# Pooling branch of a hybrid decoder mixer: means on ScalarE, ramp and subtraction on GpSimd, output matmuls at column tile 13

## The chip, the core and the metric

The kernel runs on one core of one Trainium2 chip. A core has five engines with a queue each: TensorE (PE, matmuls), VectorE (DVE), ScalarE (ACT), GpSimd (POOL) and SyncE (SP), which here issues the loads of all weights. Each engine works through its own queue in order and waits at semaphores for others. TensorE writes to PSUM (eight banks, handed out in this kernel by four pools, pa, pb, pt and pd); the other tiles lie in SBUF. The metric is the device time of one execution in microseconds (us).

## The reference

Two layers for 256 tokens of width 1,024 in float32. Each layer is a token mixer followed by a mixture of experts (32 experts, all of whose weights are streamed). The change touches the mixer, and of it the pooling branch:

```python
proj = h @ w_in[l]                                  # 1024 -> 3584 columns
u_conv = proj[..., :2 * D_CONV]                     # 2 x 512: the convolution branch
u_pool = proj[..., 2 * D_CONV:2 * D_CONV + D_POOL]  # 512: the pooling branch
gate_a, gate_b = jnp.split(jax.nn.sigmoid(proj[..., 2 * D_CONV + D_POOL:]), N_BRANCHES, axis=-1)
y_a = conformer_conv_branch(...)                    # GLU, 31 causal taps, layer norm, silu, w_conv_out
y_b = pool_branch(u_pool, pool_w[l], pool_scale[l])
x = x + g1[:, None, :] * ((gate_a * y_a + gate_b * y_b) @ w_out[l])

def pool_branch(u, pool_w, pool_scale):
    # four groups of 128 channels, windows 2, 4, 8, 16; at token s the count is min(s + 1, w)
    pooled = jnp.stack([causal_window_mean(ug[:, :, gi], w) for gi, w in enumerate(POOL_WINDOWS)], axis=2) - ug
    y = jnp.einsum("bsgc,gco->bsgo", pooled, pool_w).reshape(b, s, D_MODEL)
    return y * pool_scale
```

## The kernel before

Activations lie transposed, channels on the 128 partitions and 256 tokens along the free dimension. Weights come through a ring of 13 SBUF buffers of 1 MB (tiles `wt`, two more buffers `wx` during the experts), loaded by SP in a fixed stream; `done(key)` (L125) gives a buffer back and lets the next load be issued.

The projection is cut into 14 column tiles n = 0 to 13, each with two halves (L598 to L603). Matmuls on float32 weights are made of three faster ones: the weight is split into a rounded part `whi` (ScalarE, L444) and a residual `wlo` (GpSimd, for a few halves VectorE, L446), and `mm3` (L382) issues three matmuls for each product. `do_split(n + 2, hf)` prepares the half that comes two tiles later. The tiles run through the groups in the order 1, 0, 2, 5, 6, 3, 4 (L169), two tiles each: n = 0 to 3 is the convolution's input, n = 4 and 5 the pooling branch's (its result is `upad`, with 16 columns of zeros ahead), n = 6 to 9 the second gate (`mixed`), n = 10 to 13 the first (`ga`).

Between the halves stands the work of the two branches, in program order, since the four compute engines are scheduled by hand here (L587); only the queue of SP is ordered by the compiler's own scheduler.

- `conv` (L493) spreads 31 taps over four channel groups, 124 steps on VectorE (L503, L505), each multiplying a shifted window of `vpad` by a column and adding it to an accumulator in PSUM. The accumulators hold two of the three banks of the pool pd; the last four steps write `acc` in SBUF.
- `pool_sum(i)` (L513) builds window sums on GpSimd at n = 6 to 9, `pool_mean(i)` (L521) the means at n = 7 to 10 on VectorE: one instruction for the tokens from 16 on (L525), and for the first 16, where the count ramps up, a product with the reciprocals `rc16` (L528) and a subtraction (L529).
- `pool_out(m2)` (L531) multiplies by the pooling weights: two matmuls (L535) into a bank of pd (m2 even) or pt (m2 odd), read by two instructions of VectorE that merge them into `mixed` (L539). Two calls follow each half of n = 11.
- After n = 11 `flush` (L301) runs what is pending of the adaLN gate: two matmuls (L337) into pd, each copied by ScalarE into `gb` (L338). `gb` has the buffer that `upad` had.
- After n = 12 `ln_a` (L548) adds up `acc` on VectorE (tile `lt`, L544, L545) and takes the mean over channels by a matmul with ones (L551). `ln_b` (L558) stands within the last half of n = 13, `ln_c` (L572) behind it, after the first six matmuls of a later adaLN part (`lates`, L320). The rest of these covers the time until the layer norm's result (`ah`, `al`) is there for the matmuls with w_conv_out.

Of the kernel before, what the change touches and what calls it, by code (L numbers as in the profile page):

```python
# [7 lines left out]
F32 = mybir.dt.float32  # L8
# [4 lines left out]
AF = mybir.ActivationFunctionType  # L13
OP = mybir.AluOpType
# [4 lines left out]
P = 128  # L19
# [7 lines left out]
WINDOWS = (2, 4, 8, 16)  # L27
# [22 lines left out]
def trunk(ctx, tc, x, c, mixer_norm_g, w_ada, b_ada, w_in, conv_w, conv_b, conv_ln_g, conv_ln_b,  # L50
# [3 lines left out]
    nc = tc.nc  # L54
# [3 lines left out]
    two = ctx.enter_context(tc.tile_pool(name="two", bufs=2))  # L58
# [14 lines left out]
    def pd(shape):  # L73
        return psD.tile(shape, F32, name="pd", tag="pd")
# [50 lines left out]
    def done(key):  # L125
        finished.add(key)
        while state["done"] + 1 < len(stream) and stream[state["done"] + 1][0] in finished:
            state["done"] += 1
        issue()
# [104 lines left out]
    rc16 = cst.tile([P, 4, 16], F32, name="rc16")  # L234
# [152 lines left out]
    def mixer(l, mix, norm, g1):  # L387
# [7 lines left out]
        def transpose_x():  # L395
            hps.extend((pa, pb)[kp % 2]([P, 2, SEQ]) for kp in range(4))
            for tt in range(TT):
                v = xn[:, tt, :].rearrange("p (m k) -> p k m", k=KC)
                for k in range(KC):
                    nc.tensor.transpose(hps[k // 2][:, k % 2, tt * P:(tt + 1) * P], v[:, k, :], ident)  # L400
# [14 lines left out]
        def divide(kp):  # L415
            f = st["f", kp]
            ks = slice(2 * kp, 2 * kp + 2)
            nc.scalar.copy(hT[:, 0, ks, :], f)  # L418
            eng = nc.vector if kp in DIV_DVE else nc.gpsimd
            eng.tensor_tensor(hT[:, 1, ks, :], f, hT[:, 0, ks, :].bitcast(F32), op=OP.subtract)  # L420

        vpad = work.tile([P, 4, 30 + SEQ], F32, name="vpad")
        upad = work.tile([P, 4, 16 + SEQ], F32, name="upad", tag="gb")
        nc.gpsimd.memset(vpad[:, :, :30], 0.0)
        nc.gpsimd.memset(upad[:, :, :16], 0.0)
        st = {}
# [83 lines left out]
        def pw_of(i):  # L510
            return st["pw"][:, 3:7] if i % 2 else st["pw"][:, 0:4]

        def pool_sum(i):  # L513
            if i == 0:
                st["pw"] = work.tile([P, 7, n16], F32, name="pw", tag="hT")
            prev = pw_of(i - 1) if i else upad
            d = 1 << i
            lo = (1, 3, 7, 16)[i]
            nc.gpsimd.tensor_tensor(pw_of(i)[:, i:, lo:], prev[:, i:, lo:], prev[:, i:, lo - d:n16 - d], op=OP.add)

        def pool_mean(i):  # L521
            if i == 0:
                st["pooled"] = work.tile([P, 4, SEQ], F32, name="pooled", tag="t1")
            cur = pw_of(i)
            nc.vector.scalar_tensor_tensor(st["pooled"][:, i, 16:], cur[:, i, 32:], 1.0 / WINDOWS[i], upad[:, i, 32:],  # L525
                                           op0=OP.mult, op1=OP.subtract)
            f = two.tile([P, 16], F32, name="f16")
            nc.vector.tensor_tensor(f, cur[:, i, 16:32], rc16[:, i, :], op=OP.mult)  # L528
            nc.vector.tensor_tensor(st["pooled"][:, i, :16], f, upad[:, i, 16:32], op=OP.subtract)  # L529

        def pool_out(m2):  # L531
            pw = tiles["pw", l]
# [54 lines left out]
        with tc.manual_schedule(engines={E.PE, E.DVE, E.Activation, E.Pool}):  # L587
            transpose_x()
            for step in START[l]:
                if isinstance(step, tuple):  # L590
                    do_split(*step)
                elif step < 4:
                    modulate(step)
                else:
                    divide(step - 4)
            sg = work.tile([P, 4, SEQ], F32, name="sg", tag="t1")
            acc = mix.tile([P, 4, SEQ], F32, name="acc")
            for n in range(14):  # L598
                if n == 6:
                    st["mixed"] = work.tile([P, 8, SEQ], F32, name="mixed", tag="X0")  # L600
                if n == 10:
                    st["ga"] = work.tile([P, 8, SEQ], F32, name="ga", tag="hT")
                for hf in range(2):  # L603
                    mms(n, hf, ln_b if (n, hf) == (13, 1) else None)
                    if n == 0 and hf == 1:
                        vec_cols(l)
                    if n == 11:
                        for m2 in (2 * hf, 2 * hf + 1):
                            pool_out(m2)
                        if hf:  # L610
                            done(("pw", l))
                    if (n, hf) == (13, 1):
                        for _ in range(6):
                            next(lates)
                        ln_c()
                    conv(2 * n + hf)
                    if hf == 0 and 7 <= n <= 10:
                        pool_mean(n - 7)
                    do_split(n + 2, hf)
                    if hf == 0 and 6 <= n <= 9:  # L620
                        pool_sum(n - 6)
                if n == 12:
                    ln_a()
                evac(n)
                if n % 2:
                    flush(2 if n < 11 else None)
                if n == 0:
                    for _ in g1:
                        pass
                if n == 7 and l + 1 < DEPTH:  # L630
                    small_ada(l + 1)
            for _ in lates:
                pass
            mhl = work.tile([P, 2, 8, SEQ], F32R, name="mhl", tag="big")
            ah, al = st["ah"], st["al"]

            cps = [(pa if q % 2 == 0 else pb)([P, 2, SEQ]) for q in range(4)]
            mt4 = mix.tile([P, 4, SEQ], F32, name="mt4", tag="acc")

            def mixed_a(m2):  # L640
                for q in (2 * m2, 2 * m2 + 1):
                    t = mt4[:, q % 4, :]
                    nc.vector.scalar_tensor_tensor(t, cps[q // 2][:, q % 2, :], s["bo"][:, q:q + 1], st["ga"][:, q, :],
                                                   op0=OP.add, op1=OP.mult)
                    nc.gpsimd.tensor_tensor(t, st["mixed"][:, q, :], t, op=OP.add)

            def mixed_b(m2):
                for q in (2 * m2, 2 * m2 + 1):
                    t = mt4[:, q % 4, :]
                    nc.scalar.copy(mhl[:, 0, q, :], t)  # L650
                    nc.vector.tensor_tensor(mhl[:, 1, q, :], t, mhl[:, 0, q, :].bitcast(F32), op=OP.subtract)

            for i in range(2):
                for m in range(8):
                    hi, lo = sp[14 + i, m // 4]
                    ms = slice(m % 4 * P, (m % 4 + 1) * P)
                    for jj in range(2):
                        j = 2 * i + jj
                        mm3(cps[m // 2][:, m % 2, :], hi[:, jj, ms], lo[:, jj, ms], ah[:, j, :], al[:, j, :],
                            j == 0 and m % 2 == 0, j == 3)  # L660
                    if i == 1 and m % 2:
                        mixed_a(m // 2)
                        if m > 1:
                            mixed_b(m // 2 - 1)
                    if m % 4 == 3:
                        do_split(16 + i, m // 4)
                if i == 0:
                    flush()
            ps = [[pd([P, 512]), pd([P, 512])], [pd([P, 512]), pt([P, 512])]]

            def out_mm(i, tt, hs=range(2)):
                ts = slice(tt * P, (tt + 1) * P)
                for h in hs:
                    hi, lo = sp[16 + i, h]
                    for mm in range(2):
                        m = 2 * i + mm
                        mm3(ps[tt][h], mhl[:, 0, m, ts], mhl[:, 1, m, ts], hi[:, mm, :], lo[:, mm, :], m == 0, m == 7)

            def out_add(tt, hs=range(2)):
                for h in hs:  # L680
                    hs = slice(h * 512, (h + 1) * 512)
                    t = two.tile([P, 512], F32, name="ot", tag="part", bufs=3)
                    nc.vector.tensor_tensor(t, ps[tt][h], s["g1"][:, hs], op=OP.mult)
                    nc.vector.tensor_tensor(xs[:, tt, hs], xs[:, tt, hs], t, op=OP.add)

            for i in range(2):
                for tt in range(TT):
                    out_mm(i, tt)
                if i == 0:
                    do_split(18, 0)  # L690
                    do_split(18, 1)
                    mixed_b(3)
                    do_split(19, 0)
                    do_split(19, 1)
            router_prep(l)
# [555 lines left out]
```

## Time and profile before

| what | us |
|---|---|
| runs of the kernel before, median (lowest to highest) | 916.63 (912.15 to 921.05) |
| the profiled execution | 921.07 |
| its span, first to last instruction | 919.3 |
| busy: TensorE | 838.3 (91%) |
| busy: VectorE | 539.7 (59%) |
| busy: ScalarE | 287.2 (31%) |
| busy: GpSimd | 207.6 (23%) |
| moved by DMA | 298.35 MB, 325 GB/s in the mean |

The busy shares are means over stages of different kinds. In the experts' stages TensorE works almost without a pause while DMA streams at about 400 GB/s; in the mixers VectorE and GpSimd carry much more of the work. So the stretch around the change is read by itself: times in the rows are microseconds from the span's start, the mixer of layer 0 runs its column tiles from about 40 to 160, that of layer 1 from about 480 to 600.

### The profile page before, as it was taken

What the parts mean: (1) busy time and instruction counts of PE and PEld (TensorE: products, weight loads), DVE (VectorE), ACT (ScalarE), POOL (GpSimd) and SP (SyncE); (2) the same over time, 40 slices, a digit from 0 to 9 for tenths busy, and PEclk for the clock granted to TensorE, in tenths of its full rate; (3) what the DMA queues carried; (4) which work ended last, traced back from release to release, by engine and by line L of the source; (5) the groups of instructions that cost most, each with busy time, mean ns of one, the idle gap of its engine ahead of it and who ended that gap; (6) DMA issues with size and microseconds to landing.
All of it is one profiled execution on the core that took longest, in us unless ns stands there. A gap on an engine that the chain in (4) does not pass through costs nothing. (4 is left out here: it accounts for less than half of the span.)

```text
span 919.3 us, 12760 instructions
## 1 busy us (share of the span) xinstructions
PE 838.3 (91%) x4862; PEld 517.5 (56%) x4862; DVE 539.7 (59%) x1134; ACT 287.2 (31%) x462; POOL 207.6 (23%) x140
## 2 busy tenths in 40 slices
PE   4699939999998999999979993999899799999996
PEld 1489917864544544545349992787554454545442
DVE  2379993786443545454476999468644354535354
ACT  2254314633321222222135440364432122222222
POOL 1279912632000000000025892243200000000001
PEclk9699959999999999999989997899799999999998
DMA  9999734969999999999999752396699999999961
GB/s 349 368 365 395 282 109 146 375 239 357 408 408 407 407 400 313 406 408 409 403 373 384 280 173 102 122 402 227 221 352 409 360 357 409 409 409 409 359 225 46
DMA packets 100086, 298.35 MB, mean 325 GB/s; under 512 B 13941, under 2 KB 23461, under 8 KB 100010
## 3 DMA queue, kind: packets, MB, share of 16 engines
q1 hardware_dynamic: 99448, 296.30, 85.4%
q8 instruction: 44, 0.72, 0.3%
q10 hardware_dynamic: 434, 1.06, 0.3%
q14 instruction: 32, 0.26, 0.1%
q0 software_dynamic: 128, 0.02, 0.0%
HBM read 296.29 MB, written 1.05 MB: 323 GB/s over the span
## 5 line engine op out<-in xcount | busy, mean ns | idle before, releaser
L1095 PE MATMUL pb<-wt,XT 128*64 128x512 f32 x928 | 226.4, 592 | 0.0
L446 POOL TENSOR_TENSOR wlo<-wt,whi 128x1024 fp32r<-128x1024 f32 x60 | 147.2, 2464 | 140.2 <-ACT whi L444 117.2
L1095 PEld LDWEIGHTS pb<-wt,XT 128*64 128x64 f32 x928 | 72.8, 137 | 131.7 <-issue 129.0
L444 ACT CAST whi<-wt 128x1024 fp32r<-128x1024 f32 x80 | 83.0, 1049 | 99.1 <-PE pb L384 50.9
L505 DVE SCALAR_TENSOR_TENSOR pd<-vpad,cols,pd 128x256 f32<-128x256 f32 x232 | 108.0, 488 | 5.7
L1108 DVE SCALAR_TENSOR_TENSOR sl<-sl,ws,pb 128x256 f32<-128x256 f32 x32 | 15.4, 480 | 153.4 <-ACT sl L1107 153.4
L1055 DVE TENSOR_TENSOR xs<-xs,pd 128x512 f32<-128x512 f32 x124 | 84.2, 683 | 33.0 <-PE pd L1048 32.9
L1067 PE MATMUL pd<-wt,aT 128*64 128x512 f32 x448 | 102.3, 598 | 0.0
L1074 ACT CAST yhl<-y 128x512 fp32r<-128x512 f32 x64 | 39.5, 618 | 132.9 <-DVE y L1073 132.9
L1020 ACT ACTIVATE XT<-pa,B,A 128x256 f32<-128x256 f32 x112 | 57.1, 559 | 67.4 <-PE pa L1015 67.1
L383 PE MATMUL pa<-hhl,whi 128*128 128x256 f32 x224 | 68.8, 307 | 5.3 <-ACT hhl L418 5.3
L320 PE MATMUL pd<-wt,cb 128*32 128x512 f32 x384 | 55.4, 664 | 14.4 <-DMA wt<-in_w_ada_dram 14.4
L1078 DVE TENSOR_TENSOR yhl<-y,yhl 128x512 fp32r<-128x512 f32 x64 | 44.3, 692 | 41.1 <-ACT yhl L1074 41.0
L384 PE MATMUL pa<-hhl,whi 128*128 128x256 f32 x224 | 67.2, 300 | 0.3
L1107 ACT ACTIVATE sl<-pb 128x256 f32<-128x256 f32 x32 | 12.3, 384 | 175.4 <-PE pb L1095 160.0
L1015 PEld LDWEIGHTS pa<-G,xhl 128*128 128x128 f32 x448 | 62.4, 193 | 7.7 <-issue 2.7
L1015 PE MATMUL pa<-G,xhl 128*128 128x256 f32 x448 | 64.7, 288 | 2.2 <-issue 2.2
L385 PE MATMUL pa<-hhl,wlo 128*128 128x256 f32 x224 | 66.1, 295 | 0.5 <-POOL wlo L446 0.5
L383 PE MATMUL pb<-hhl,whi 128*128 128x256 f32 x224 | 63.6, 284 | 0.0
L384 PE MATMUL pb<-hhl,whi 128*128 128x256 f32 x224 | 62.7, 280 | 0.0
L385 PE MATMUL pb<-hhl,wlo 128*128 128x256 f32 x224 | 62.6, 279 | 0.0
L1047 PE MATMUL pd<-yhl,GT 128*128 128x512 f32 x124 | 56.1, 453 | 6.0 <-PEq L953 5.4
(251 smaller groups left out, 1353.8 us busy)
## 6 DMA issues: line engine op xcount, KB each, us to landing
wt<-in_w_expert_gate_dram SPq DMA_DIRECT2D x116, 512.0 KB, 8.2
wt<-in_w_expert_up_dram SPq DMA_DIRECT2D x116, 512.0 KB, 10.9
wt<-in_w_expert_down_dram SPq DMA_DIRECT2D x52, 1024.0 KB, 10.7
wt<-in_w_ada_dram SPq DMA_DIRECT2D x48, 1024.0 KB, 10.9
wt<-in_w_in_dram SPq DMA_DIRECT2D x28, 1024.0 KB, 13.6
wt<-in_w_out_dram SPq DMA_DIRECT2D x8, 1024.0 KB, 4.9
wx<-in_w_expert_down_dram SPq DMA_DIRECT2D x8, 1024.0 KB, 10.6
wx<-in_w_expert_gate_dram SPq DMA_DIRECT2D x12, 512.0 KB, 3.7
```

The lines of the kernel that those rows point to most:

```text
L383: nc.tensor.matmul(o, ah, bh, start=start, stop=False, skip_group_check=True)
L384: nc.tensor.matmul(o, ah, bl, start=False, stop=False, skip_group_check=True)
L385: nc.tensor.matmul(o, al, bh, start=False, stop=stop, skip_group_check=True)
L444: nc.scalar.copy(hi, wv)
L446: eng.tensor_tensor(lo, wv, hi.bitcast(F32), op=OP.subtract)
L505: nc.vector.scalar_tensor_tensor(acc[:, j, :] if t == CONV_K - 1 else a, src, w, a, op0=OP.mult, op1=OP.add)
L1015: nc.tensor.matmul(p[:, kk, :], xhl[:, q, tt, k * P:(k + 1) * P], Gs[ch][:, tt, :], start=i == 0, stop=i == 3)
L1020: nc.scalar.activation(XTs[ch][:, k, :], p[:, kk, :], AF.Identity, bias=s["B2"][:, k:k + 1], scale=s["A2"][:, k:k + 1])
L1047: nc.tensor.matmul(o, GTs[b][:, tt, :], ys[b][0][:, hs], start=True, stop=False)
L1055: nc.vector.tensor_tensor(xs[:, tt, hs], xs[:, tt, hs], outs.pop(part), op=OP.add)
L1067: nc.tensor.matmul(o[64 * j:64 * j + 64, :], aTs[b][:, h, 64 * j:64 * j + 64], wv[j][:, h, :], start=h == 0, stop=h == 1)
L1095: nc.tensor.matmul(p[64 * j:64 * j + 64], XT[:, k, so + 64 * j:so + 64 * j + 64], w[j][:, :, kk, :], start=k == 0, stop=k == KC - 1)
```

## The change

The mean of the tokens from 16 on is taken on ScalarE, a copy with a scale, into `pooled`. A new function `pool_diff`, called once after the second half of n = 10, does the rest on GpSimd: four products for the first 16 tokens and one subtraction of `upad` over all four groups, in place. The output matmuls of `pool_out` and the release of the pooling weights follow the halves of n = 13 instead of n = 11. `ga`, whose buffer the window sums `pw` use, is allocated one tile later.

```diff
         def pool_mean(i):
             if i == 0:
                 st["pooled"] = work.tile([P, 4, SEQ], F32, name="pooled", tag="t1")
-            cur = pw_of(i)
-            nc.vector.scalar_tensor_tensor(st["pooled"][:, i, 16:], cur[:, i, 32:], 1.0 / WINDOWS[i], upad[:, i, 32:],
-                                           op0=OP.mult, op1=OP.subtract)
-            f = two.tile([P, 16], F32, name="f16")
-            nc.vector.tensor_tensor(f, cur[:, i, 16:32], rc16[:, i, :], op=OP.mult)
-            nc.vector.tensor_tensor(st["pooled"][:, i, :16], f, upad[:, i, 16:32], op=OP.subtract)
+            nc.scalar.activation(st["pooled"][:, i, 16:], pw_of(i)[:, i, 32:], AF.Copy, scale=1.0 / WINDOWS[i])
+
+        def pool_diff():
+            v = st["pooled"]
+            for i in range(4):
+                nc.gpsimd.tensor_tensor(v[:, i, :16], pw_of(i)[:, i, 16:32], rc16[:, i, :], op=OP.mult)
+            nc.gpsimd.tensor_tensor(v, v, upad[:, :, 16:], op=OP.subtract)
...
-                if n == 10:
+                if n == 11:
                     st["ga"] = work.tile([P, 8, SEQ], F32, name="ga", tag="hT")
...
-                    if n == 11:
+                    if n == 13:
                         for m2 in (2 * hf, 2 * hf + 1):
                             pool_out(m2)
...
                     if hf == 0 and 6 <= n <= 9:
                         pool_sum(n - 6)
+                    if (n, hf) == (10, 1):
+                        pool_diff()
```

Lines behind the edit move down by one to three: L535, L539, L544, L551 and L576 of before are L536, L540, L545, L552 and L577 of the changed kernel.

VectorE's queue in layer 0 before, from the long run of convolution steps to the sum `lt` (the other three means and their steps are left out between the pieces):

```order
L505 SCALAR_TENSOR_TENSOR pd<-vpad,cols,pd 128x256 x40
L525 SCALAR_TENSOR_TENSOR pooled<-pw,upad 128x240
L528 TENSOR_TENSOR f_860<-pw,rc_116 128x16
L529 TENSOR_TENSOR pooled<-f_860,upad 128x16
L505 SCALAR_TENSOR_TENSOR pd<-vpad,cols,pd 128x256 x12
...
L505 SCALAR_TENSOR_TENSOR pd<-vpad,cols,pd 128x256 x6
L539 SCALAR_TENSOR_TENSOR mixed<-pd,cols,mixed 128x256 x2
L539 SCALAR_TENSOR_TENSOR mixed<-pt,cols,mixed 128x256 x2
L505 SCALAR_TENSOR_TENSOR pd<-vpad,cols,pd 128x256 x4
L505 SCALAR_TENSOR_TENSOR acc<-vpad,cols,pd 128x256 x4
L544 TENSOR_TENSOR lt<-acc 128x512
L545 TENSOR_TENSOR lt<-lt 128x256
```

The same place of the changed kernel, down to the last step of the layer norm:

```order
L505 SCALAR_TENSOR_TENSOR pd<-vpad,cols,pd 128x256 x92
L505 SCALAR_TENSOR_TENSOR acc<-vpad,cols,pd 128x256 x4
L545 TENSOR_TENSOR lt<-acc 128x512
L546 TENSOR_TENSOR lt<-lt 128x256
L553 SCALAR_TENSOR_TENSOR acc<-pd,acc 128x1024
L545 TENSOR_TENSOR lt<-sq 128x512
L546 TENSOR_TENSOR lt<-lt 128x256
L540 SCALAR_TENSOR_TENSOR mixed<-pd,cols,mixed 128x256 x2
L540 SCALAR_TENSOR_TENSOR mixed<-pt,cols,mixed 128x256 x2
L446 TENSOR_TENSOR wlo_279<-wt,whi_278 128x1024
L565 TENSOR_SCALAR ve<-pt 128x2
L570 TENSOR_SCALAR rb<-ones,rs_1317 128x128 x2
```

The pooling instructions have left the convolution's run, and the merging into `mixed` stands behind both sums of the layer norm, four of its eight instructions ahead of the variance `ve` and four behind the scale `rb`.

GpSimd's queue of the changed kernel, from the last window sum on (`wlo_277` and `wlo_279` are the two buffers that the residuals take in turn):

```order
L519 TENSOR_TENSOR pw<-pw 128x256
L446 TENSOR_TENSOR wlo_279<-wt,whi_278 128x1024
L446 TENSOR_TENSOR wlo_277<-wt,whi_276 128x1024 x2
L529 TENSOR_TENSOR pooled<-pw,rc_116 128x16 x4
L530 TENSOR_TENSOR pooled<-pooled,upad 128x1024
L446 TENSOR_TENSOR wlo_279<-wt,whi_278 128x1024 x2
```

The five instructions L529 and L530 are new; before, the last two residuals followed the two ahead of them at once.

## Rows read from the trace of the kernel before

**Rows 1.** The page, first part: busy us and share of the span.

```profile
PE 838.3 (91%) x4862; PEld 517.5 (56%) x4862; DVE 539.7 (59%) x1134; ACT 287.2 (31%) x462; POOL 207.6 (23%) x140
```

**Rows 2.** TensorE's waits, whole span: waiter <- releaser: us, times, longest.

```profile
PE pd L535 <- DVE mixed L539: 27.4, 2, 13.7
...
PE pa L830 <- DVE G L897: 2.0, 1, 2.0
```

**Rows 3.** TensorE's timeline, layer 0: start, us, instruction [idle before <- releaser].

```profile
106.47 0.28 PE L383 MATMUL pa<-hhl,whi 128*128 128x256 f32 x1
...
109.30 1.02 PE L535 MATMUL pd<-pooled,wt 128*128 128x256 f32 x4
...
129.29 2.08 PE L535 MATMUL pd<-pooled,wt 128*128 128x256 f32 x4 [13.69 <-DVE mixed L539]
...
136.35 2.07 PE L337 MATMUL pd<-part,Q 128*128 128x512 f32 x2 [0.67 <-ACT gb L338]
...
145.43 0.59 PE L551 MATMUL pd<-lt,ones 128*128 128x256 f32 x2
...
154.69 6.20 PE L320 MATMUL pd<-wt,cb 128*32 128x512 f32 x52
```

**Rows 4.** Groups by line and form, VectorE: count, busy us, mean ns, idle before.

```profile
L525 DVE SCALAR_TENSOR_TENSOR pooled<-pw,upad 128x240 f32<-128x240 f32 x8 | 15.2, 1901 | 0.0
L528 DVE TENSOR_TENSOR f<-pw,rc 128x16 f32<-128x16 f32 x8 | 10.2, 1271 | 0.0
L529 DVE TENSOR_TENSOR pooled<-f,upad 128x16 f32<-128x16 f32 x8 | 7.2, 905 | 0.3
```

**Rows 5.** VectorE's timeline, layer 0.

```profile
73.76 19.90 DVE L505 SCALAR_TENSOR_TENSOR pd<-vpad,cols,pd 128x256 f32<-128x256 f32 x40
...
98.88 5.58 DVE L505 SCALAR_TENSOR_TENSOR pd<-vpad,cols,pd 128x256 f32<-128x256 f32 x12
...
119.51 5.59 DVE L505 SCALAR_TENSOR_TENSOR pd<-vpad,cols,pd 128x256 f32<-128x256 f32 x12
125.00 0.40 DVE L525 SCALAR_TENSOR_TENSOR pooled<-pw,upad 128x240 f32<-128x240 f32 x1
...
137.77 0.69 DVE L544 TENSOR_TENSOR lt<-acc 128x512 f32<-128x512 f32 x1
138.49 0.42 DVE L545 TENSOR_TENSOR lt<-lt 128x256 f32<-128x256 f32 x1
...
159.95 0.42 DVE L583 TENSOR_TENSOR al<-acc,ah 128x256 fp32r<-128x256 f32 x1 [0.51 <-ACT ah L582]
```

**Rows 6.** Two stretches: PE, PEld, DVE, ACT, POOL busy, granted clock, DMA share, GB/s.

```profile
118.00:142.00 24.00, 11.50 (x31) 7.63 (x32) 20.28 (x48) 2.26 (x4) 1.03 (x1) 0.51 0.25 88
657.00:661.00 4.00, 3.93 (x20) 3.74 (x22) 2.08 (x6) 1.26 (x3) 0.00 (x0) 0.57 0.51 208
```

**Rows 7.** GpSimd: window sums and residuals, from its groups by line and its timeline.

```profile
L519 POOL TENSOR_TENSOR pw<-upad 128x1084 f32<-128x1084 f32 x2 | 4.0, 1990 | 0.0
...
103.61 0.74 POOL L519 TENSOR_TENSOR pw<-pw 128x256 f32<-128x256 f32 x1
104.31 9.57 POOL L446 TENSOR_TENSOR wlo<-wt,whi 128x1024 fp32r<-128x1024 f32 x4
```

**Rows 8.** ScalarE's timeline: the cast for tile 12 and a copy of gb.

```profile
103.80 1.05 ACT L444 CAST whi<-wt 128x1024 fp32r<-128x1024 f32 x1 [0.76 <-POOL wlo L446]
...
135.72 0.58 ACT L338 COPY gb<-pd 128x512 f32<-128x512 f32 x1 [9.11 <-PE pd L337]
```

**Rows 9.** SP's wait for the pooling weights' buffer; one wx load, landing times, its use.

```profile
SPq L115 <- PE pt L535: 13.6, 1, 13.6
...
229.15 0.42 SPq L113 DMA_DIRECT2D wx<-in_w_expert_up_dram  x1
...
DMA to landing us min/median/max: 5.6/12.8/13.3
...
255.58 0.59 PE L1095 MATMUL pb<-wx,XT 128*64 128x512 f32 x1
```

## What the change does to the time: the prediction

> **What bounds the kernel now.** I read the page's first part, then who waited for whom on TensorE, then the timelines of the stretch where it waited. TensorE is busy 838.3 of 919.3 us [rows 1], so what is to be won lies in its idle time. The largest entry among its waits is 27.4 us in two pieces, 13.7 the longer, one in each layer: matmuls of the pooling branch (L535) stand until VectorE has run L539 [rows 2]. No expert matmul (L1095, L1067) is in that list with a wait for weights.
>
> The timeline of layer 0 shows how it comes about [rows 3]. Column tile 11 has two halves; the first starts at 106.47 and gives way to L535 at 109.30, so a half takes 2.83. Then come four records of L535, some of the next, the second half, and at 129.29, after 13.69 us of nothing, the third four. They need a pd bank. The convolution's accumulators hold two of the three, and the third comes free only when VectorE reaches L539. VectorE is that late because its queue holds 96 convolution steps (0.465 each in the batches of twelve [rows 5]) and, between them, the pooling means. In both layers these took 15.2, 10.2 and 7.2 us, 16.3 a layer, at means of 1.90, 1.27 and 0.90 [rows 4], although the last L525 of layer 0, which ran when GpSimd had nothing to do, took 0.40 [rows 5]. By the Trainium skill (SBUF — State Buffer, Who interferes with whom), a VectorE instruction with two SBUF inputs and a GpSimd instruction that reads SBUF exclude each other for a whole instruction; the trace agrees, with its 1.90 against 0.40.
>
> The idle time costs twice. From 118 to 142 the granted clock is 0.51, the 1.2 GHz level [rows 6], after TensorE had stood from 115.6 on: four records of L535 take 2.08 there instead of 1.02, and an L337 takes 2.07, so 1.03 at the higher level [rows 3]. So the mean of the layer normalization (L551) starts at 145.43, and meanwhile VectorE in turn waits for TensorE: its sum lt was done at 138.91 [rows 5].
>
> **The change part by part** (times of layer 0; layer 1 repeats the pattern, its long wait as well).
>
> *VectorE, removed.* All twelve pooling instructions, and the eight L539 that stood before lt, each of a convolution step's size. Nothing is left between the 96 steps, and these never waited. The first 40 end at 93.7 (73.76 + 19.90), 56 more at 0.465 end at 119.7, and the sum's two steps, 0.69 and 0.42 [rows 5], put lt at 120.8, 18 us sooner.
>
> *GpSimd, added.* Four products of 16 columns and one subtraction of 1,024, behind the second residual of tile 12. No row shows these. A line through the window sums on the same engine, 0.74 at 256 columns and 1.99 at 1,084 [rows 7], gives 0.38 and 1.90, so 3.4 in all. From below it is 1.9 (products at nothing), from above 5.4 (each product 0.74, the subtraction 2.39 like wlo). I take 3.4: same operation, same tiles. It starts when the third of four wlo from 104.31 ends, 104.31 + 3 x 2.39 = 111.5, and ends at 114.9. Behind it stand both wlo of tile 13, now done at 119.7; TensorE wants them after 122, which hides the delay. Without that cover it costs 3.4 a layer.
>
> *ScalarE, added.* Four means of 240 columns, each between nothing and the 0.58 of the 512-column copy [rows 8]. Each stands ahead of a whi cast and waits for its window sum. The last sum ends at 104.35, where the cast had begun at 103.80; now it ends at 104.35 + 0.58 + 1.05 = 106.0, before GpSimd is through with the wlo in hand, 104.31 + 2.39 = 106.7 [rows 7, 8]. Cost nothing; without that cover 4 x 0.58 a layer.
>
> *The new wait.* gb lies in the buffer of upad, so its copy (L338) can't start before GpSimd's subtraction is done, and the second L337 needs the one free pd bank, which the copy empties. Tile 11 ends at 112.1 (109.30 + 2.83), the first L337 at 113.2; the copy runs from 114.9 to 115.5, the second L337 ends at 116.5. TensorE idles 2.3 us here instead of the 13.7. An idle 2.0 us before L830 [rows 2] was followed by 4 us at a granted 0.57 [rows 6], 1.7 us of lost work; I charge that too, between nothing and 6.2 (rival 1). Behind the copy on ScalarE stands the cast for tile 14, wanted later.
>
> *TensorE.* Tile 12 takes 2 x 2.83, to 122.2, or 123.9 with the clock's 1.7. lt is there, so L551 starts at 123.9, 21.5 us sooner. From there the old sequence follows with the sixteen L535 records in it, at 1.02 for four: 4.1. Net 17.4 us a layer.
>
> *The layer normalization's tail.* VectorE gets the eight L539 into this chain, 8 x 0.465 = 3.7, and TensorE the 4.1 of L535 ahead of the same point. The last al ended at 160.37 [rows 5], the w_ada matmuls that cover it at 160.89 [rows 3]; that margin of 0.5 stays. Uncovered it would cost 3.7.
>
> *SP and DMA.* The release of the pooling weights moves from tile 11 to tile 13. SP stood 13.6 us for it [rows 9]; it now comes at about 134 (123.9 and some 10 of matmuls), no later than before (some 4 behind 129.29 [rows 3]), for w_out tiles that no cast wants yet. Two of an extra buffer's 512 KB loads go behind twelve more tiles. That buffer's last load was issued at 229.15, at most 13.3 us before landing, and was used at 255.58 [rows 9]: 13 us of cover. Cost nothing; bounded by the landing time, 13.3, if the cover were gone.
>
> Sum: 2 x 17.4 = 34.8. The profiled execution took 921.07 us, 919.3 of them its span: 886.3. It lies at the top of the runs shown (912.15 to 921.05); from their median, 4.4 lower, it is 881.8. **I predict 884**, between the two; the rivals are priced from there.
>
> **A rule weighed.** A pooling step of 240 columns averages 1.90 us on VectorE [rows 4], a window sum of 256 takes GpSimd 0.74 [rows 7]. By the Trainium skill (GPSIMD Engine Reference, Engine selection) elementwise work on two inputs belongs on VectorE, GpSimd being about twice as slow. That speaks against this change, and holds for 0.40 against 0.74 alone. By the rows the sum is 884; by the rule the time taken from VectorE is worth no more than its lone price, which is rival 3 and 901.
>
> **Rivals.**
> 1. *GpSimd is late.* The five instructions take 5.4, 2.0 more of waiting, and the clock behaves as after the long stall, at its lower level from 129.3 to 142: 6.2 us of lost work instead of 1.7. That is 6.5 a layer, 897. For it: GpSimd's queue runs without a gap from 104 on. Against: the window sums' times.
> 2. *The wait moves to lt.* Its two sums read SBUF twice and may each be held for a whole wlo of 2.39. Then lt comes at 125.6, 1.7 after TensorE wants it, and the clock takes another 4.5: 896. For it: 1.90 against 0.40. Against: wlo of tile 13 ends at 119.7, as the sums begin, and wlo of tile 14 needs the first half of tile 12 to be through.
> 3. *VectorE gets back only the lone price.* If the rest of the pooling's time goes over to the convolution steps, VectorE wins at most 12 x 0.40 = 4.8 of the 16.3. lt comes at 132.3, L551 13.1 sooner; less 4.1, 9.0 a layer: 901. Against: twelve steps beside a busy GpSimd and twelve beside an idle one took 5.58 and 5.59 [rows 5].
> 4. *Slower: GpSimd's residuals stretch.* The convolution now runs without the pauses in which VectorE stood at a pooling step. If GpSimd lived off these, each wlo of tiles 4 to 13 would be held: twice as long, 4.78, exceeds TensorE's 2.83 by 1.95, for twenty halves 39 a layer, 962. It decides at 2.83 + 17.4 / 20 = 3.7 us a wlo. Against: 2.39 beside convolution steps [rows 5, 7].
> 5. *No change: the weights set the end*, and the time won is spent waiting for them: 919. For it: DMA ran at 0.25 in the stall [rows 6], a time to catch up that goes. Against: SP stood for buffers in it, not for transfers [rows 9].
>
> **How the numbers follow.** Forecast 0.67, rivals 0.13, 0.08, 0.05, 0.03 and 0.04. The forecast's own range is 875 to 890: no clock loss gives back 3.4, the subtraction and products at their lower bound 3.0, and the runs shown lie 4.5 to either side of their median. The range goes from 874 to 898, with rivals 1 and 2 inside and 0.12 left out. Faster by over 1% (about what a measurement can tell from no change) are the forecast and rivals 1 to 3: 0.93; within 1% rival 5, 0.04; slower rival 4, 0.03.
>
> **What would show it.** Right: 92 steps of L505 in one run, lt near 121; no wait of L536 above 1 us; one wait of about 2.3 before the second L337, for ScalarE's copy; L552 near 124; a granted clock near 1.0 over most of 118 to 142. Wrong: products on GpSimd above 1 us; waits of TensorE for lt or al above 1 us; expert matmuls that wait for DMA; convolution steps above 0.47, or wlo above 2.5.

## The result and the profile after

The changed kernel takes 881.59 us (median; 879.98 to 881.93), the kernel before beside it 916.35 (912.15 to 921.05): a ratio of 0.962 (0.957 to 0.966). A second measurement on another occasion gave 882.11 and 0.961 (0.957 to 0.966). The prediction was 884, in a range of 874 to 898. The spans of the two profiled executions are 919.3 and 879.9, 39.4 apart, the medians 34.8, since the profiled execution of the kernel before lies at the top of its runs. The prediction's sum was 34.8.

The page's first part, as in [rows 1]:

```profile
PE 827.1 (94%) x4862; PEld 513.0 (58%) x4862; DVE 510.1 (58%) x1110; ACT 289.8 (33%) x470; POOL 213.5 (24%) x150
```

VectorE's busy time fell by 29.6, with 24 instructions fewer; GpSimd and ScalarE carry 5.9 and 2.6 more. TensorE does the same number of instructions; it idles 28.2 less and is busy 11.2 less, at a mean granted clock of 0.970 instead of 0.945.

TensorE's waits, as in [rows 2] (waiter <- releaser: us, times, longest):

```profile
PE pd L320 <- DMA wt<-in_w_ada_dram: 14.2, 5, 6.4
...
PE pd L337 <- ACT gb L338: 4.0, 2, 2.0
```

The 27.4 us of [rows 2] are gone; the pooling matmuls (now L536) are not in the list. In their place stands the wait before the second L337 that the prediction named, 2.0 in each layer. No expert matmul waits for its weights.

TensorE's timeline in layer 0, the place of [rows 3]:

```profile
112.26 1.02 PE L337 MATMUL pd<-part,Q 128*128 128x512 f32 x2
...
115.28 1.12 PE L337 MATMUL pd<-part,Q 128*128 128x512 f32 x2 [1.99 <-ACT gb L338]
...
123.40 0.59 PE L552 MATMUL pd<-lt,ones 128*128 128x256 f32 x2
...
126.65 1.03 PE L536 MATMUL pd<-pooled,wt 128*128 128x256 f32 x4
127.52 1.03 PE L536 MATMUL pt<-pooled,wt 128*128 128x256 f32 x4
...
135.99 6.20 PE L320 MATMUL pd<-wt,cb 128*32 128x512 f32 x52
```

The mean of the layer normalization (L552) starts at 123.40 where L551 started at 145.43: 22.0 sooner. The last w_ada matmuls (L320), which cover the layer norm's tail, end at 142.19 instead of 160.89, 18.7 sooner; the same point of layer 1 comes 38.8 sooner. So 38.8 of the span's 39.4 are won by the end of the second mixer.

VectorE, in the stretch of [rows 5]:

```profile
83.64 33.76 DVE L505 SCALAR_TENSOR_TENSOR pd<-vpad,cols,pd 128x256 f32<-128x256 f32 x73
...
118.99 0.82 DVE L545 TENSOR_TENSOR lt<-acc 128x512 f32<-128x512 f32 x1
119.84 0.42 DVE L546 TENSOR_TENSOR lt<-lt 128x256 f32<-128x256 f32 x1
124.03 1.23 DVE L553 SCALAR_TENSOR_TENSOR acc<-pd,acc 128x1024 f32<-128x1024 f32 x1 [3.76 <-PE pd L552]
...
141.25 0.43 DVE L584 TENSOR_TENSOR al<-acc,ah 128x256 fp32r<-128x256 f32 x1 [0.51 <-ACT ah L583]
```

The convolution runs without a pause, 0.462 a step; lt is done at 120.26 and VectorE then waits 3.76 for TensorE. The last `al` ends at 141.68, 0.51 ahead of the w_ada matmuls' end; before it was 0.52.

GpSimd and ScalarE, to be held against [rows 7] and [rows 8]:

```profile
104.29 7.16 POOL L446 TENSOR_TENSOR wlo<-wt,whi 128x1024 fp32r<-128x1024 f32 x3
111.37 0.81 POOL L529 TENSOR_TENSOR pooled<-pw,rc 128x16 f32<-128x16 f32 x4
112.25 2.35 POOL L530 TENSOR_TENSOR pooled<-pooled,upad 128x1024 f32<-128x1024 f32 x1
114.56 4.71 POOL L446 TENSOR_TENSOR wlo<-wt,whi 128x1024 fp32r<-128x1024 f32 x2
121.85 2.40 POOL L446 TENSOR_TENSOR wlo<-wt,whi 128x1024 fp32r<-128x1024 f32 x1 [2.59 <-ACT whi L444]
...
104.39 0.41 ACT L524 ACTIVATE pooled<-pw 128x240 f32<-128x240 f32 x1 [1.22 <-POOL pw L519]
...
114.64 0.59 ACT L338 COPY gb<-pd 128x512 f32<-128x512 f32 x1 [0.21 <-POOL pooled L530]
```

The four products take 0.81 together, the subtraction 2.35; it ends at 114.60 and the copy of `gb` starts at once.

Two stretches by engine, as in [rows 6] (the granted clock is the number after POOL's):

```profile
118.00:142.00 24.00, 24.00 (x178) 17.35 (x176) 13.01 (x25) 10.01 (x14) 6.77 (x4) 0.96 0.56 202
118.00:122.00 4.00, 4.00 (x29) 4.00 (x28) 2.20 (x5) 1.05 (x1) 1.41 (x2) 0.74 0.37 110
```

From 118 to 142 the granted clock is 0.96 instead of 0.51; what is missing lies right behind the wait of 1.99. SP's wait for the pooling weights' buffer, 13.6 in [rows 9], is now 6.1.

### The profile page after: what moved, and what is told of

Same layout as the page of the kernel before. It is cut to its first block, busy times and chain, and to the rows that moved or that the text cites. A ratio compares the mean times of both kernels' runs of the same rounds, so it can differ in the third digit from the quotient of the medians.

```text
span 879.9 us, 12744 instructions
## 1 busy us (share of the span) xinstructions
PE 827.1 (94%) x4862; PEld 513.0 (58%) x4862; DVE 510.1 (58%) x1110; ACT 289.8 (33%) x470; POOL 213.5 (24%) x150
## 5 line engine op out<-in xcount | busy, mean ns | idle before, releaser
L383 PE MATMUL pa<-hhl,whi 128*128 128x256 f32 x224 | 67.5, 301 | 5.3 <-ACT hhl L418 5.3
L320 PE MATMUL pd<-wt,cb 128*32 128x512 f32 x384 | 53.7, 644 | 14.2 <-DMA wt<-in_w_ada_dram 14.2
L384 PE MATMUL pa<-hhl,whi 128*128 128x256 f32 x224 | 66.4, 297 | 0.3
L1018 PEld LDWEIGHTS pa<-G,xhl 128*128 128x128 f32 x448 | 62.2, 193 | 6.5 <-issue 1.7
L1018 PE MATMUL pa<-G,xhl 128*128 128x256 f32 x448 | 64.7, 287 | 0.9 <-issue 0.9
L1050 PE MATMUL pd<-yhl,GT 128*128 128x512 f32 x124 | 56.4, 454 | 6.2 <-PEq L956 5.6
## 6 DMA issues: line engine op xcount, KB each, us to landing
wt<-in_w_in_dram SPq DMA_DIRECT2D x28, 1024.0 KB, 13.6
```

The source lines that it names most:

```text
L383: nc.tensor.matmul(o, ah, bh, start=start, stop=False, skip_group_check=True)
L384: nc.tensor.matmul(o, ah, bl, start=False, stop=False, skip_group_check=True)
L1018: nc.tensor.matmul(p[:, kk, :], xhl[:, q, tt, k * P:(k + 1) * P], Gs[ch][:, tt, :], start=i == 0, stop=i == 3)
L1050: nc.tensor.matmul(o, GTs[b][:, tt, :], ys[b][0][:, hs], start=True, stop=False)
```

## The experiments

Two theories were to be told apart at first. Mine: the gain needs both halves of the change, because VectorE's pooling steps are long only where GpSimd holds them, and because the output matmuls ask for a bank that VectorE frees late. The rival: one half alone is enough, the later place of the matmuls above all, since the wait of [rows 2] is theirs. Where nothing else is said, each edit is to the changed kernel.

**The later place alone** (edit to the kernel before; the means stay on VectorE):

```diff
-                    if n == 11:
+                    if n == 13:
                         for m2 in (2 * hf, 2 * hf + 1):
                             pool_out(m2)
```

> The kernel before with one edit: the output matmuls at tile 13. Means, ramp and subtraction stay on VectorE. My theory: VectorE's lateness is the cause, so the wait only moves. The copy of gb now waits for the last pooling step on VectorE (about 125.7 in layer 0), TensorE idles some 12 us before the second L337 and gets the lower clock; L551 starts near 136 instead of 145.4, less 4.1 for the moved matmuls: about 5 us a layer, 907 (902 to 911). Rival (the place alone decides, since at tile 13 the banks are free): 882 to 886.

Measured 911.96, ratio 0.995 (0.991 to 0.999). TensorE, VectorE and GpSimd, timelines of layer 0:

```profile
125.42 2.08 PE L337 MATMUL pd<-part,Q 128*128 128x512 f32 x2 [12.21 <-ACT gb L338]
138.16 1.19 PE L551 MATMUL pd<-lt,ones 128*128 128x256 f32 x2 [3.87 <-DVE lt L545]
...
132.91 2.60 DVE L544 TENSOR_TENSOR lt<-acc 128x512 f32<-128x512 f32 x1
135.55 2.46 DVE L545 TENSOR_TENSOR lt<-lt 128x256 f32<-128x256 f32 x1
...
132.59 2.38 POOL L446 TENSOR_TENSOR wlo<-wt,whi 128x1024 fp32r<-128x1024 f32 x1 [16.24 <-ACT whi L444]
135.39 2.34 POOL L446 TENSOR_TENSOR wlo<-wt,whi 128x1024 fp32r<-128x1024 f32 x1 [0.42 <-ACT whi L444]
```

The wait only moves: the copy of `gb` needs the buffer of `upad`, which VectorE reads to its last pooling step, so TensorE stands 12.21 one step later. Then lt's two sums, two SBUF inputs each, take 2.60 and 2.46 instead of 0.69 and 0.42: GpSimd runs one residual from 132.59 to 134.97 and the next from 135.39 to 137.73, and each sum ends 0.3 to 0.5 behind one of them. That is 4.0 a layer; TensorE waits 3.87 for it, and L551 starts at 138.16 where I expected 136, which covers most of the 5 us above what I expected. The rival falls, and what the prediction's second rival feared has occurred, in another kernel.

**The early place kept** (means and subtraction moved, output matmuls back at tile 11):

```diff
-                    if n == 13:
+                    if n == 11:
                         for m2 in (2 * hf, 2 * hf + 1):
                             pool_out(m2)
```

> The changed kernel with the output matmuls back at tile 11. My theory: without the pooling steps VectorE reaches the merging at about 112.7, so the 13.7 us for the bank go, but the matmuls now wait for GpSimd's subtraction (114.6) from 109.4 on: 5 us of idle time with the lower clock behind it, and the last convolution steps stand behind the merging. L552 near 131 to 133: 13 us a layer gained, 890 to 893. Rival (VectorE's time alone decides): 882 or less, since the eight instructions of the merging no longer stand in the layer norm. Rival (the place alone decides): about 917.

Measured 892.73, ratio 0.974 (0.968 to 0.979). TensorE, layer 0:

```profile
112.76 2.08 PE L536 MATMUL pd<-pooled,wt 128*128 128x256 f32 x4 [4.99 <-POOL pooled L530]
...
130.12 0.59 PE L552 MATMUL pd<-lt,ones 128*128 128x256 f32 x2
```

This half alone is worth 25.3 beside its own kernel before (917.99), the other alone 6.0, both together 35.9: most lies in VectorE's relief. By these medians 4.6 come only with both; the intervals of the ratios are too wide to show that. At tile 11 the matmuls wait for GpSimd, 4.99, instead of for VectorE.

**Products and subtraction on VectorE**, at the same place:

```diff
-                nc.gpsimd.tensor_tensor(v[:, i, :16], pw_of(i)[:, i, 16:32], rc16[:, i, :], op=OP.mult)
-            nc.gpsimd.tensor_tensor(v, v, upad[:, :, 16:], op=OP.subtract)
+                nc.vector.tensor_tensor(v[:, i, :16], pw_of(i)[:, i, 16:32], rc16[:, i, :], op=OP.mult)
+            nc.vector.tensor_tensor(v, v, upad[:, :, 16:], op=OP.subtract)
```

> The changed kernel with the four products and the subtraction on VectorE instead of GpSimd, at the same place of the program (behind 82 convolution steps, about 112.7 in layer 0). My theory: each has two SBUF inputs and is held beside GpSimd's residuals, products at up to 1.27 (their mean in the kernel before), the subtraction at 1.2 to 3.6: ended near 119 to 121, lt near 127 to 128.5 instead of 120.3, L552 4 to 5 us later in each layer: 889 to 892. Rival (VectorE is the better engine for such work, 0.17 a product and 1.2 for the subtraction): ended at 114.6, lt at 122.2, hidden: 881 to 882.

Measured 891.35, ratio 0.974 (0.967 to 0.981). VectorE and TensorE, layer 0:

```profile
112.69 3.55 DVE L529 TENSOR_TENSOR pooled<-pw,rc 128x16 f32<-128x16 f32 x4
116.34 1.23 DVE L530 TENSOR_TENSOR pooled<-pooled,upad 128x1024 f32<-128x1024 f32 x1
...
118.30 2.08 PE L337 MATMUL pd<-part,Q 128*128 128x512 f32 x2 [5.10 <-ACT gb L338]
```

Four instructions of 16 columns take 3.55, some 0.9 each; on GpSimd they take 0.81 together. The subtraction is quicker on VectorE, 1.23 against 2.35, yet ends at 117.57 instead of 114.60: the products start 1.3 later, behind convolution steps, and take 2.7 longer. So the wait before the second L337 is 5.10 instead of 1.99. The time is 9.2 above the 882.11 of the kernel as changed, which is given below and was measured on another occasion; the kernel before took 917.0 here and 918.0 there.

**The means on VectorE**, with one SBUF input and a scalar:

```diff
-            nc.scalar.activation(st["pooled"][:, i, 16:], pw_of(i)[:, i, 32:], AF.Copy, scale=1.0 / WINDOWS[i])
+            nc.vector.tensor_scalar(st["pooled"][:, i, 16:], pw_of(i)[:, i, 32:], 1.0 / WINDOWS[i], None, op0=OP.mult)
```

> The changed kernel with the four means on VectorE as multiplications by a constant, with one SBUF input, instead of ScalarE. My theory: with one SBUF input they are not held beside GpSimd's residuals, some 0.35 each; lt moves from 120.3 to 121.7, still ahead of TensorE at 123.4: 881 to 883. Rival: they are held as the two-input means were, 1.9 each, lt near 128, 4.5 us a layer: 890 to 891.

Measured 891.54, ratio 0.974 (0.967 to 0.981). VectorE, then GpSimd, layer 0:

```profile
93.38 2.17 DVE L524 TENSOR_SCALAR pooled<-pw 128x240 f32<-128x240 f32 x1
...
100.97 0.39 DVE L524 TENSOR_SCALAR pooled<-pw 128x240 f32<-128x240 f32 x1
...
106.77 2.42 DVE L524 TENSOR_SCALAR pooled<-pw 128x240 f32<-128x240 f32 x1
...
114.61 0.28 DVE L524 TENSOR_SCALAR pooled<-pw 128x240 f32<-128x240 f32 x1
...
93.00 4.82 POOL L446 TENSOR_TENSOR wlo<-wt,whi 128x1024 fp32r<-128x1024 f32 x2
...
98.81 4.81 POOL L446 TENSOR_TENSOR wlo<-wt,whi 128x1024 fp32r<-128x1024 f32 x2
...
104.28 7.19 POOL L446 TENSOR_TENSOR wlo<-wt,whi 128x1024 fp32r<-128x1024 f32 x3
```

I had thought that one input frees the instruction from GpSimd; it doesn't. Cut each group of wlo into equal parts, and a wlo ends at 95.41, at 101.21 and at 109.07; the first three means end at 95.55, 101.36 and 109.19, 0.12 to 0.15 later each. The fourth, beside an idle GpSimd, takes 0.28. So a mean on VectorE ends when the GpSimd instruction of that moment does, and its length is whatever is left of that. The fourth stands behind convolution steps until 114.61, and GpSimd's subtraction waits 2.84 for it; the second L337 then waits 4.88.

**The place of the subtraction on GpSimd**: one half tile later, and one earlier.

```diff
-                    if (n, hf) == (10, 1):
+                    if (n, hf) == (11, 0):
                         pool_diff()
```

> The opposite of the earlier subtraction: products and subtraction one half later, behind the first residual of tile 13. My theory: the subtraction ends near 117.0 instead of 114.6, the wait before the second L337 grows from 2.0 to 4.4, and the lower clock lasts longer (between 1.7 and 6.2 us of lost work): 2.4 to 7 us a layer, 887 to 895. Rival: covered, 881 to 882.

Measured 887.94, ratio 0.969 (0.962 to 0.976); L552 starts at 125.82. TensorE, layer 0:

```profile
117.63 2.08 PE L337 MATMUL pd<-part,Q 128*128 128x512 f32 x2 [4.34 <-ACT gb L338]
```

And with `(10, 0)`:

> The subtraction and the four products on GpSimd stand one half earlier, after the first half of tile 10 instead of the second. My theory: what is left of the wait (1.99 us before the second L337, and a granted clock below 1.0 behind it) comes from the copy of gb that waits for this subtraction. GpSimd then ends it near 112.2 instead of 114.6, before the first L337 is done, the wait goes, and the layer norm's mean (L552) starts when lt is there, at about 120.5 instead of 123.4: some 3 us a layer, 875 to 876 against 881.6. Rival: the remaining wait is covered by something behind it (the tail of the layer norm), or the residual of tile 12, now 3.2 us later, holds TensorE instead: 881 or more.

Measured 878.49, ratio 0.958 (0.954 to 0.962). ScalarE and TensorE, layer 0:

```profile
112.33 1.04 ACT L444 CAST whi<-wt 128x1024 fp32r<-128x1024 f32 x1 [1.78 <-POOL pooled L530]
113.28 0.59 ACT L486 ACTIVATE ga<-pa 128x512 f32<-128x512 f32 x1
113.77 0.59 ACT L486 ACTIVATE ga<-pb 128x512 f32<-128x512 f32 x1
114.25 0.59 ACT L338 COPY gb<-pd 128x512 f32<-128x512 f32 x1
...
114.89 1.12 PE L337 MATMUL pd<-part,Q 128*128 128x512 f32 x2 [1.68 <-ACT gb L338]
```

The subtraction is done at 112.26, but the copy of `gb` stands behind a cast and two evacuations in ScalarE's queue, so the wait shrinks only to 1.68. The granted clock from 118 to 124 is 1.00 here (0.83 as changed), and L552 starts at 121.45, 1.95 sooner. A wait of 1.7, 2.0 and 4.3 goes with 878.5, 882.1 and 887.9. The ratios of neighbours overlap, but L552 moves in the same order, 121.45, 123.40 and 125.82: the wait before L337 is on the path. The prediction's first rival priced it too high, though: 6.5 a layer for 2.0 more of waiting, where 2.35 more cost 5.8 in all, 2.9 a layer. The clock lost no more for it: from 110 to 142 it is 0.95 with the later subtraction and 0.95 as changed.

**As changed, once more**, beside these:

> The changed kernel again, beside the others on the same chip: 881.6 expected, a ratio of 0.962 to the kernel before.

882.11 (879.51 to 884.12).

**The wait taken away.** Before the last runs my theory was that this wait and the clock behind it are all that the new dependence costs. The second L337 gets a bank of the pool pt and no longer waits for the copy:

```diff
-                    p = pd([P, 512])
+                    p = (pt if h and m == 2 else pd)([P, 512])
                     nc.tensor.matmul(p, Q[:, h, :], part, start=True, stop=True)
```

> The changed kernel, with the second L337 of the gate after tile 11 written to a bank of pt, so that it does not wait for the copy of gb. Theory (the wait of 1.99 and the 3.4 us at the lower clock behind it are all that the new dependence costs): no wait at L337, granted clock near 1.0 over tile 12, L552 at 120.4, where lt (120.3) sets it instead of TensorE; 3.0 us sooner a layer, 876 (874 to 878). Rival (the copy's lateness matters on ScalarE, whose cast for tile 14 stands behind both copies, or the clock falls for another reason): 880 to 883, L552 still after 122.5.

Measured 884.87 (880.97 to 887.63), ratio 0.963 (0.959 to 0.967): no gain, and the theory falls. VectorE, GpSimd and TensorE, layer 0, and one stretch by engine:

```profile
119.00 1.10 DVE L545 TENSOR_TENSOR lt<-acc 128x512 f32<-128x512 f32 x1
120.14 2.45 DVE L546 TENSOR_TENSOR lt<-lt 128x256 f32<-128x256 f32 x1
...
114.79 10.04 POOL L446 TENSOR_TENSOR wlo<-wt,whi 128x1024 fp32r<-128x1024 f32 x4
...
122.74 0.67 PE L552 MATMUL pd<-lt,ones 128*128 128x256 f32 x2 [2.76 <-DVE lt L546]
...
124.00:142.00 18.00, 18.00 (x129) 12.22 (x129) 9.45 (x19) 6.98 (x11) 1.53 (x2) 0.92 0.52 189
```

L337 doesn't wait any more and tile 12 ends at 120.0. But with TensorE earlier, ScalarE's cast for tile 14 comes earlier (117.14 instead of 120.72), and GpSimd goes straight on with the next residual. As changed it was idle from 119.3 to 121.85, for nearly all of lt's sums; now the second sum is held, 2.45 instead of 0.42, TensorE waits 2.76 for it, and the clock drops to 0.92 in the stretch behind. The wait that I removed had kept that residual back.

The same with the subtraction one half tile earlier, and that earlier place alone, on the same occasion:

> The bank of pt as in the run before, and the subtraction on GpSimd one half tile earlier. Theory: TensorE no longer waits for the subtraction in either kernel and VectorE's convolution run (lt at 120.3) sets L552, so the earlier place adds nothing: 876 (874 to 878), the same as without it. Rival (the two edits remove different pieces): 872 to 873.

> The subtraction one half tile earlier alone, on the chip of the two runs above: 878 to 879, L552 at 121.4, a wait of 1.7 at L337; by the theory 2 us slower than the run with the bank of pt.

882.37 (ratio 0.962, 0.958 to 0.966) and 878.16 (0.956, 0.952 to 0.959). The first is longer than both its theory and its rival had it, and the bank of pt, which I thought worth 2 us, costs 4.2 between these two. With the bank of pt the sum L546 takes 2.45 again and L552 waits 2.76; without it the wait of 1.68 stays and the whole is faster.

**lt with one sum less.** If the held sum is what eats the gain, taking it away must bring it. To the kernel with the bank of pt and the early subtraction:

```diff
-            t = total(acc)
+            t = two.tile([P, 2, SEQ], F32, name="lt", tag="part", bufs=3)
+            nc.vector.tensor_tensor(t, acc[:, :2, :], acc[:, 2:, :], op=OP.add)
             pm = pd([P, SEQ])
-            nc.tensor.matmul(pm, ones, t, start=True, stop=True)
+            for j in range(2):
+                nc.tensor.matmul(pm, ones, t[:, j, :], start=j == 0, stop=j == 1)
```

> The run with the bank of pt and the early subtraction, with the second of lt's two sums left to TensorE (two matmuls with ones instead of a sum and one matmul). Theory (what cancelled the gain there is that lt's second sum, with two inputs in SBUF, waits for a wlo of GpSimd, 2.45 instead of 0.42): lt done at 119.9, the mean's matmuls start at 120.0 when tile 12 ends, no wait there above 0.3, granted clock 1.0 over 118 to 142, two matmul records more (0.45); 1.5 to 2.5 sooner a layer, 877 to 879. Rival (the place of TensorE's pause is not what matters there): 882, as without the edit.

Measured 879.77, ratio 0.962 (0.957 to 0.966): about as long as expected, but not in the way expected. VectorE and TensorE, layer 0:

```profile
119.36 1.35 DVE L551 TENSOR_TENSOR lt<-acc 128x512 f32<-128x512 f32 x1
...
120.85 2.04 PE L554 MATMUL pd<-lt,ones 128*128 128x256 f32 x4 [2.58 <-DVE lt L551]
```

Here TensorE reached that point at 118.3, 1.5 sooner than with both sums on VectorE, and still waited 2.58: for the convolution itself, which ended at 119.3, and for the first sum, 1.35 instead of 0.69. In layer 1 the wait is 0.27.

TensorE is sooner here from the projection's start, 34.17 instead of 36.55, because a small step ahead of it was not held. L349, 128x8 on VectorE with two SBUF inputs, started at 32.27 and took 0.17; GpSimd's residual started at 32.28. In the kernel with both sums L349 started at 32.50, GpSimd's residual at 32.45, and L349 took 2.31. The edit doesn't touch that place, and the kernel with the output matmuls at tile 11 has the short L349 too (0.17). So a start some hundredths of a us earlier or later decides over 2.1 us, and this run alone doesn't say what one sum less is worth.

**No sum on VectorE at all**: four matmuls with ones over `acc` in place of `total(acc)` and one matmul.

> As the run before, with both of lt's sums left to TensorE: four matmuls with ones over acc, no sum on VectorE ahead of the mean. Theory: the mean's matmuls start at 119.9 whatever GpSimd does, six records more than one matmul (1.3); about 878, within 1 of the run with one sum. Rival: 882.

Measured 872.98 (871.21 to 874.56), ratio 0.954 (0.950 to 0.958): the fastest of all. TensorE, layer 0:

```profile
113.01 1.02 PE L337 MATMUL pt<-part,Q 128*128 128x512 f32 x2
...
119.48 1.89 PE L552 MATMUL pd<-acc,ones 128*128 128x256 f32 x8
```

And of the kernel with both sums (bank of pt, early subtraction), from TensorE's waits over the whole span:

```profile
PE pd L552 <- DVE lt L546: 5.5, 2, 2.8
...
PE pa L1018 <- issue: 1.3, 1, 1.3
```

With no sum ahead of the mean TensorE has no wait of L337 or L552 in either layer, and a granted clock of 1.00 from 110 to 142. The mean starts at 119.48 instead of 122.57, and six records more cost 1.3. So the held sum was what kept the gain of the free bank back. Its profiled span is 8.7 shorter than with both sums (878.8): 4.8 of it by the end of the second mixer, and most of the rest behind it, from 680 to 720, where the granted clock is 1.00 here and 0.91 there, 3.6 of 40. My expectation counted the first part only.

That second part can't be put down to the edit. It lies in the experts, where TensorE stands a second time, 1.3 before the L1018 shown (from 692.5 on), shortly after a wait before L1050. The other traces all have that pause, 0.9 us or more (L1015 in the kernel before); only this one has none, and nothing here shows why. Against the earlier place of the subtraction alone (878.16, span 876.4) the second mixer ends 2.1 sooner, and the ratios (0.954, 0.950 to 0.958, against 0.956, 0.952 to 0.959) don't tell the two apart.

## Why the prediction was right, step by step

The mechanism was right, the wait that replaces the old one included; in the size some errors cancel.

- *The bound.* Right: with VectorE relieved the wait for the bank is gone, and no other of its size comes up. That VectorE was late because GpSimd held its pooling steps is shown by the means on VectorE (2.17 and 2.42 against 0.28) and by the four products on VectorE (0.9 each against 0.17, the length of an L528 beside an idle GpSimd in the run with the later place alone).
- *VectorE, removed.* Right: 96 steps in one run, lt at 120.26 (predicted 120.8). The third rival, that only the lone price comes back, would have put it at 132.3.
- *GpSimd, added.* Right in the sum, 3.2 for 3.4, by two errors that cancel in part, which is luck: a product takes 0.20 where the line gave 0.38, the subtraction 2.35 where it gave 1.90. It ended at 114.60 (114.9). The fourth rival falls: wlo stays at 2.39 beside the convolution.
- *ScalarE.* Right: 0.41 a mean, and no wait of TensorE follows from it.
- *The new wait.* Right in place, cause and size: 1.99 for 2.3. The clock: from the second L337 to L552 it takes 8.12 as changed, 6.56 with the earlier subtraction, where the clock doesn't fall; so 1.56 for the 1.7 charged.
- *L552.* 123.40 for 123.9.
- *The pooling matmuls behind it.* Mis-sized: 4.1 for the sixteen records (the profile has two for one matmul here). From L552 to the end of the w_ada matmuls it took 15.46 before and takes 18.79 now, 3.3 more. Four records last 1.03, but the next four start 0.87 behind them: the records overlap, and I added durations where starts were to be subtracted.
- *The tail.* Right: the margin is 0.51, before 0.52. SP and DMA: right, SP's wait fell to 6.1 and nothing waits for it.
- *The sum.* Layer 0 gained 18.7 for 17.4, 0.8 of the rest by the pooling matmuls and 0.5 by the earlier L552. Layer 1 gained 20.1, but 1.6 of it ahead of the change's part: ScalarE begins the evacuation of tile 9 at 102.10 instead of 101.96 in layer 0, and at 522.73 instead of 543.05 in layer 1. From there to the end of the w_ada matmuls the gain is 18.8 and 18.5. So between the profiled executions the sum is low by 4.6. Between the medians (916.35 and 881.59) it is exact, and that is luck: terms of it are off as said, and the profiled execution of the kernel before lies 4.7 above its median, for which no trace shows the place. Taken from between the two, 884 came out 2.4 high.
- *The second rival* did not occur as changed, but only in part for the reason I gave. GpSimd's next residual does need the first half of tile 12 to be through, as I argued; but it was the wait at L337 and the low clock behind it that kept that half back long enough, which I had not said. With the bank of pt, which takes that wait away, lt is held, with the early subtraction and without it. So the step was right by a margin of 1.6 us that I had not worked out: lt was done at 120.26, GpSimd's next residual began at 121.85.
- *The rule weighed* (the Trainium skill, GPSIMD Engine Reference, Engine selection: elementwise work on two inputs belongs on VectorE) gives the better place only for an instruction by itself: 1.23 against 2.35 for the subtraction. Beside a busy GpSimd the products cost four times as much on VectorE, and the whole 9.2 us.

## What to carry to other kernels

Price a VectorE instruction by what GpSimd does at that moment. Here sums, products and scalings of tiles in SBUF could last until GpSimd's present instruction ended, however short they were; the convolution steps, which read one window from SBUF and the accumulator from PSUM, did not (0.462 each in a run beside GpSimd's residuals). So GpSimd's own queue or another engine may be the cheaper place for such an instruction even if it takes longer there. When a wait goes away, look at what it had held back: here removing it set a residual going just where a sum on the path needed the same access, and nothing was won by it until that sum was moved too. After a move, look up who last reads a buffer that something else reuses; that, not the moved work itself, made the new wait.

## What was not expected of the hardware

An instruction of VectorE with a single SBUF input, a scaling of 240 float32 columns, is held as well: 2.17 and 2.42, against 0.28 beside an idle GpSimd and 0.39 where GpSimd's instruction was near its end. The Trainium skill (SBUF — State Buffer, Who interferes with whom) has `tensor_scalar` among the operations that can come to use the ports shared with GpSimd, in certain modes; the traces agree with that, though no row shows the mode.

Whether the clock falls doesn't follow from the length of one wait alone. A wait of 1.68 before L337 was followed by a granted clock of 1.00, one of 1.99 at the same place by 0.74 from 118 to 122. Before an expert's L1050 TensorE stood 2.65 in the fastest kernel, and the clock stayed at 1.00; it stood 2.62 there in the second run of the early subtraction, and the clock was 0.91 from 680 to 720. What the traces show beside that is the second pause: in this run TensorE stood 1.24 more, until 691.06, and the clock was 0.54 from 690 to 692 and 0.50 from 692 to 696; the fastest kernel has no such pause. What else decides stays open.
